# High and low halves in one stationary operand, and 512-column products in the second layer: a two-block network on one core

## The chip, the cores and the metric

The kernel runs on one core of a Trainium2 chip. The metric is the device time of one execution in microseconds; the time before is the median of three runs. The profile is one further execution, recorded instruction by instruction. Its engines are TensorE (PE, with its weight loads as PEld), VectorE (DVE), ScalarE (ACT), GpSimd (POOL) and SyncE (SP), which issues the loads.

## What is computed

Two blocks follow each other on 512 tokens of width 1024. The first has 16 extra meta tokens in front (528 rows) and two layers; the second has chunked attention over 8 heads, a gated recurrence, cross attention to a memory, and 32 routed experts. What the change touches, cut from the reference:

```python
for l in range(DEPTH):                       # first block, DEPTH = 2
    u = rms_norm(h, norm_w[l]) @ w_in[l]
    f_in, f_gate, p_in, p_gate, c_q, c_kv, k_r, a_gate = split(u)
    y_f, y_p = fourier_mix(f_in), pool_mix(p_in)
    y_a = mla_mix(c_q, c_kv, k_r, ...)       # k_r, 64 wide, is the rope key shared by 4 heads
    mix = concat(y_f*silu(f_gate), y_p*silu(p_gate), y_a*silu(a_gate))
    h = h + mix @ w_out[l]
...
probs = softmax(q @ k.T / 8 + bias)          # second block: 8 heads of 64 columns
out = probs @ v
```

## The kernel before

Every fp32 product is made of three TensorE products. An operand is split into a high part (rounded to the PE's input type) and a low part (what the rounding left), and `mm3` (L182) adds high x high, high x low and low x high in PSUM. Weights are split in `weights` (L162): ACT writes the high part at L176, POOL the low part at L177. Activations are split by `split` and `scaled_split` (ACT at L196 or L203, DVE at L197 or L204).

In the first block activations lie with features on partitions and tokens in the free dimension. `proj_g` computes one output tile of 128 features for all tokens in two halves. With all 528 tokens a half is 264 columns. In the second layer (`l == 1`) the results of the meta tokens are not used, so the queries, the gates and the output projection run over 512 tokens, in two halves of 256. With `small` the halves have one-bank tiles `p`, otherwise a two-bank tile `pp`; the generator hands control back every four steps of k, so that such projections can serve as fillers in the attention loop.

The input projection of a layer runs its column blocks in the order of `todo`: three query blocks, two key/value blocks, two pooling blocks (DVE then slides windows over them in `window`, L409 to L419), the rope keys (`None`), and two Fourier blocks `f`. For the rope keys `weights` loads the 64 columns twice, so that 128 output rows hold two equal copies, 48 products in all; one DVE instruction (L356) scales them out of PSUM, `rope` makes the swapped copy with four ACT copies (L311) and three DVE operations (L312 to L314), and `split` ends it (L196, L197). After that DVE scales the two Fourier blocks (L356), whose transposes (L554) are the next thing on PE.

In the second block the values are computed for all heads into four PSUM tiles and split into `vv`, one pair of high and low tiles for each 128 tokens. `outputs(h)` (L1002 on) multiplies a 128-column pair of heads with the transposed probabilities by `mm3`, for four blocks of keys with 512, 384, 256 and 128 columns, and copies the 64 rows of its own head out of PSUM with one ACT copy (L1013). Between the scores of one item and the transposes of the one before, the loop calls `fill`, which puts other projections on PE.

A scheduler orders the instructions of each engine when the program is built; an engine then executes its own in that order, and one that waits holds all behind it on its engine.

## Time and profile before

| what | before |
|---|---|
| median of 3 runs | 1425.4 us (1424.39 to 1425.71) |
| profiled execution, its own time | 1425.72 us |
| its span | 1423.9 us |
| PE busy | 1353.4 us, 95% of the span |
| DVE, ACT, POOL busy | 48%, 39%, 31% |

In time the first block takes the span up to about 522 us (the second layer starts at about 275 us), the second block's attention and cross attention up to about 890 us, and router and experts the rest. A row of the timeline gives the start in us from the beginning of the span, the duration in us, the engine, the source line, the operation, what is written and read, how many merged instructions, and in brackets how long the engine stood idle before it and who ended the wait. PE durations contain the passage through the array, so that successive products overlap: what a product takes in a row of them is read from the distance of starts, not from its duration.

### The profile page before, as it was taken

To read this page: it belongs to the slowest core of one execution; us is meant where nothing else is said; L and a number is where in the kernel's file an instruction comes from. 1 tells how busy PE (TensorE), PEld (TensorE's weight loads), DVE (VectorE), ACT (ScalarE), POOL (GpSimd) and SP (SyncE) were. 2 spreads that over 40 slices of the span, in tenths; PEclk is the share of its full clock that TensorE was granted. 3 is DMA by queue.
4 is the path that set the end of the run, shared out by engine and by line. 5 is a ranking of instruction groups with operands and counts; after the bars stand their busy time and mean duration, and the time that the engine had idled before them with its cause. 6 is when DMAs were issued, how large, how long until landed. Compare 5 with 4: busy or idle time off the path is not lost.

```text
span 1423.9 us, 21255 instructions
## 1 busy us (share of the span) xinstructions
PE 1353.4 (95%) x8236; PEld 1018.1 (71%) x8236; DVE 683.4 (48%) x1305; ACT 555.1 (39%) x1048; POOL 440.1 (31%) x363
## 2 busy tenths in 40 slices
PE   6999999999999999989999999979999999999996
PEld 5998999999899997767876788863454354354343
DVE  5656775455677636777766244252213123132224
ACT  5355554334555562667755344421111110111113
POOL 3432223743222488464477432512000000000002
PEclk9999999999999999999999999989999999999998
DMA  6321112332211242313345122959999999999994
GB/s 202 96 75 40 49 52 84 97 97 66 56 42 58 69 125 81 90 52 120 103 127 175 38 63 91 347 200 382 423 403 423 422 422 423 422 420 422 422 418 154
DMA packets 159288, 279.32 MB, mean 196 GB/s; under 512 B 15568, under 2 KB 127440, under 8 KB 135120
## 3 DMA queue, kind: packets, MB, share of 16 engines
q1 hardware_dynamic: 159184, 277.92, 53.0%
q8 instruction: 66, 1.08, 0.3%
q14 instruction: 38, 0.31, 0.1%
HBM read 275.79 MB, written 2.10 MB: 195 GB/s over the span
## 4 chain that ended last, share of the span: by engine, by line
PE 59%; DVE 7%; DMA 3%; ACT 2%; issue 1%; POOL 1%; DVEq 0%; SPq 0%; POOLq 0%; ACTq 0%
PE pga L1530 7%; PE pgb L1530 7%; PE pm L184 5%; PE pm L185 5%; PE pm L183 5%; PE pgs L1621 4%; PE pgz L1580 3%; PE pgy L1580 3%; PE pgs L1352 3%; PE p L183 2%; PE p L184 2%; PE p L185 2%; DMA ring<-in_expert_gate_w_dram 1%; DMA ring<-in_expert_up_w_dram 1%; DVE slab L197 1%
## 5 line engine op out<-in xcount | busy, mean ns | idle before, releaser
L177 POOL TENSOR_TENSOR wl<-wraw,wh 128x512 fp32r<-128x512 f32 (+1 forms) x248 | 328.1, 1332 | 457.1 <-ACT wh L176 425.2
L176 ACT ACTIVATE wh<-wraw 128x512 fp32r<-128x512 f32 (+1 forms) x248 | 150.6, 616 | 212.6 <-PE pm L184 49.8
L183 PE MATMUL pp<-slab,wh 128*128 128x264 f32 (+1 forms) x536 | 154.8, 290 | 7.6 <-ACT wh L176 6.8
L184 PE MATMUL pp<-slab,wh 128*128 128x264 f32 (+1 forms) x536 | 155.7, 291 | 2.9 <-DVE slab L204 2.7
L185 PE MATMUL pp<-slab,wl 128*128 128x264 f32 (+1 forms) x536 | 154.8, 289 | 1.0 <-POOL wl L177 1.0
L1788 POOL TENSOR_TENSOR ring<-xtok,sel 128x512 f32<-128x512 f32 x4 | 5.0, 1282 | 406.2 <-DVE xtok L1623 406.2
L185 PE MATMUL pm<-slab,wl 128*128 128x512 f32 (+1 forms) x320 | 121.5, 381 | 5.6 <-POOL wl L177 5.5
L184 PE MATMUL pm<-slab,wh 128*128 128x512 f32 (+1 forms) x320 | 120.9, 378 | 2.2 <-DVE slab L197 2.2
L183 PE MATMUL pm<-slab,wh 128*128 128x512 f32 (+1 forms) x320 | 121.1, 380 | 0.0
L183 PE MATMUL p<-slab,wh 128*128 128x264 f32 (+1 forms) x400 | 115.7, 289 | 3.3 <-DVE rs L247 1.6
L1530 PE MATMUL pga<-ring,xT 128*64 128x512 f32 x504 | 116.1, 596 | 0.0
L1530 PE MATMUL pgb<-ring,xT 128*64 128x512 f32 x512 | 113.7, 592 | 0.3 <-DMA ring<-in_expert_up_w_dram 0.3
L185 PE MATMUL p<-slab,wl 128*128 128x264 f32 (+1 forms) x400 | 113.1, 283 | 0.0
L184 PE MATMUL p<-slab,wh 128*128 128x264 f32 (+1 forms) x400 | 112.8, 282 | 0.0
L183 PEld LDWEIGHTS pp<-slab,wh 128*128 128x128 f32 x536 | 103.6, 194 | 8.0 <-ACT wh L176 6.8
L184 PEld LDWEIGHTS pp<-slab,wh 128*128 128x128 f32 x536 | 103.4, 193 | 4.7 <-DVE slab L204 4.2
L185 PEld LDWEIGHTS pp<-slab,wl 128*128 128x128 f32 x536 | 103.8, 194 | 1.5 <-POOL wl L177 1.5
L1530 PEld LDWEIGHTS pgb<-ring,xT 128*64 128x64 f32 x512 | 37.0, 137 | 73.6 <-issue 71.4
L1590 DVE SCALAR_TENSOR_TENSOR yl<-pgy,wcol,yh 128x512 fp32r<-128x512 f32 x16 | 12.0, 751 | 158.2 <-ACT yh L1589 158.2
L1530 PEld LDWEIGHTS pga<-ring,xT 128*64 128x64 f32 x504 | 35.4, 137 | 66.1 <-issue 65.6
L183 PEld LDWEIGHTS p<-slab,wh 128*128 128x128 f32 x400 | 75.5, 189 | 5.1 <-issue 1.7
L184 PEld LDWEIGHTS p<-slab,wh 128*128 128x128 f32 x400 | 75.4, 189 | 0.0
(412 smaller groups left out, 3007.6 us busy)
## 6 DMA issues: line engine op xcount, KB each, us to landing
ring<-in_expert_gate_w_dram SPq DMA_DIRECT2D x63, 1024.0 KB, 17.7
ring<-in_expert_up_w_dram SPq DMA_DIRECT2D x62, 1024.0 KB, 16.2
ring<-in_expert_down_w_dram SPq DMA_DIRECT2D x56, 1024.0 KB, 17.0
wraw<-in_w_in_dram SPq DMA_DIRECT2D x108, 256.0 KB, 2.9
wraw<-in_w_out_dram SPq DMA_DIRECT2D x48, 256.0 KB, 2.9
wraw<-in_xk_w_dram SPq DMA_DIRECT2D x16, 256.0 KB, 2.9
wraw<-in_xv_w_dram SPq DMA_DIRECT2D x16, 256.0 KB, 2.6
wraw<-in_xq_w_dram SPq DMA_DIRECT2D x16, 256.0 KB, 2.9
```

The source lines that it names most:

```text
L176: ACT(h, raw, AF.Copy)
L177: G.tensor_tensor(lo, raw, h.bitcast(F32), op=OP.subtract)
L183: mm(ps, lh, rh, start=first, stop=False)
L184: mm(ps, lh, rl, start=False, stop=False)
L185: mm(ps, ll, rh, start=False, stop=last)
L197: V.tensor_tensor(lo, x, h.bitcast(F32), op=OP.subtract)
L1352: mm(p, h3[:, i, 128 * k:128 * k + 128], sl_[i], start=i == 0 and z == 0, stop=i == 3 and z == 1)
L1530: mm(p[64 * z:64 * z + 64], xt[:, k, CAP * (q + z):CAP * (q + z) + 64], W(src, 2 * pr + z, k), start=k == 0, stop=k == KT - 1)
L1580: mm(ps[c // 512][64 * z:64 * z + 64, c % 512:c % 512 + n], hT_[:, k, 64 * z:64 * z + 64], W("d", 2 * pr + z, k, c, n), start=k == 0, stop ...
L1590: V.scalar_tensor_tensor(yl, p, w[:rows, 0:1], yh.bitcast(F32), op0=OP.mult, op1=OP.subtract)
L1621: mm(p, t[:, 128 * i:128 * i + 128], y, start=q == 0, stop=q == len(ys) - 1)
L1788: G.tensor_tensor(y[i][:, :512], xtok[:, i, :512], fnw[:, :512], op=OP.mult)
```

## The change

Three edits. First, `proj_g` computes a tile of 512 columns in one pass where the operand has 512 columns (`whole`), hands control back every two steps of k instead of four, and evacuates once. Second, the rope keys: `w_rope` loads the 64 columns once and writes high and low part side by side into one 128-column operand; each is multiplied with the high and the low activations, 32 products instead of 48, and the two halves of the result are added with three ACT copies and two DVE operations. Third, the values of the second block: high and low part of a head stand side by side in 128 columns, so `outputs` needs two products where it had three; the two halves of its result are added by an ACT copy and a DVE addition instead of the one ACT copy. `vv` is split by 16 instructions on 256 columns instead of 8 on 512.

```diff
             K = len(X)
-            n = (X[0][0].shape[1] - q0) // 2
+            n = X[0][0].shape[1] - q0
+            whole = n == 512
+            n, kk = (n, 2) if whole else (n // 2, 4)
...
-                    if k % 4 == 3 and k < K - 1:
+                    if k % kk == kk - 1 and k < K - 1:
                         yield
 
-            if small:
+            if whole:
+                p = p1t() if small else ppt()[:, 0]
+                yield from run(p, 0)
+                evac(p, lambda t: t)
+                yield
+            elif small:
...
+        def w_rope(l):
+
+            raw = wraw.tile([128, 512], F32, name="wraw").rearrange("p (k n) -> p k n", k=KT)
+            nc.sync.dma_start(raw, a["w_in"][l][:, 1664:1728].rearrange("(k p) n -> p k n", p=128))
+            ws = []
+            for q, nm in enumerate(("wh", "wl")):
+                t = wp.tile([128, 512], F32R, name=nm).rearrange("p (k z n) -> p k z n", k=4, z=2)
+                x = raw[:, 4 * q:4 * q + 4]
+                ACT(t[:, :, 0], x, AF.Copy)
+                G.tensor_tensor(t[:, :, 1], x, t[:, :, 0].bitcast(F32), op=OP.subtract)
+                ws += [t[:, k].rearrange("p z n -> p (z n)") for k in range(4)]
+            return ws
...
-            krh, krl = split(rope(inproj(None)))
+            kr = slab()
+            w = ahead(None)
+            p = ppt()
+            for hf in range(2):
+                for k, x in enumerate(X):
+                    for z in range(2):
+                        mm(p[:, hf, :HL], w[k], x[z][:, hf * HL:hf * HL + HL], start=k == 0 and z == 0,
+                           stop=k == KT - 1 and z == 1)
+            ACT(halves(kr)[64:], p[64:, :, :HL], AF.Copy)
+            ACT(kr[:64], kr[64:], AF.Copy)
+            V.tensor_tensor(halves(kr)[:64], p[:64, :, :HL], halves(kr)[:64], op=OP.add)
+            V.tensor_tensor(kr[:64], kr[:64], R1()[:64], op=OP.mult)
+            ACT(kr[64:], kr[:64], AF.Copy)
+            krh, krl = split(rope(kr))
...
-        vv = [scaled_split(pv[j], r12[:, j:j + 1], n=S) for j in range(4)]
+
+        vv = []
+        for j in range(4):
+            vv.append([slab(F32R, S) for _ in range(2)])
+            for q, t in enumerate(vv[j]):
+                tv = t.rearrange("p (e z c) -> p e z c", e=4, z=2)
+                scaled_split(pv[j][:, 256 * q:256 * q + 256].rearrange("p (e c) -> p e c", e=4), r12[:, j:j + 1],
+                             tv[:, :, 0], tv[:, :, 1])
...
-            c = slice(128 * pr, 128 * pr + 128)
             for j in range(4):
                 s = slice(384 * j + 128 * j, 384 * j + 512)
-                mm3(p[:, 128 * j:], vv[j][0][:, c], vv[j][1][:, c], th[:, s], tl[:, s], j == 0, j == 3)
+                v = vv[j][h // 4][:, 128 * (h % 4):128 * (h % 4) + 128]
+                mm(p[:, 128 * j:], v, th[:, s], start=j == 0, stop=False)
+                mm(p[:, 128 * j:], v, tl[:, s], start=False, stop=j == 3)
...
-            ACT(yat[pr][r], p[r], AF.Copy)
+            t = slab(n=S)
+            ACT(t[:64], p[64:], AF.Copy)
+            V.tensor_tensor(yat[pr][r], p[:64], t[:64], op=OP.add)
```

The order of DVE's instructions at the rope keys of the second layer, before; `slab` with `pp` is a scaling out of PSUM, and the last line but one is the two Fourier blocks:

```order
L418 TENSOR_TENSOR slab<-slab,tab_83 64x2x8
L419 TENSOR_TENSOR slab<-slab 64x2x8
L356 TENSOR_TENSOR slab<-pp,slab 128x528
L312 TENSOR_TENSOR slab<-slab,tab_83 128x528
L313 TENSOR_TENSOR slab<-slab,tab_83 128x528
L314 TENSOR_TENSOR slab<-slab 128x528
L197 TENSOR_TENSOR slab<-slab 128x528
L356 TENSOR_TENSOR slab<-pp,slab 128x528 x2
L197 TENSOR_TENSOR big<-pt,big 106x5x128
```

The same place in the changed kernel, where L319 to L321 are the lines of `rope` and L375 is what L356 was:

```order
L437 TENSOR_TENSOR slab<-slab,tab_83 64x2x8
L459 TENSOR_TENSOR slab<-pp,slab 64x528
L438 TENSOR_TENSOR slab<-slab 64x2x8
L460 TENSOR_TENSOR slab<-slab 64x528
L319 TENSOR_TENSOR slab<-slab,tab_83 128x528
L320 TENSOR_TENSOR slab<-slab,tab_83 128x528
L321 TENSOR_TENSOR slab<-slab 128x528
L197 TENSOR_TENSOR slab<-slab 128x528
L375 TENSOR_TENSOR slab<-pp,slab 128x528 x2
L197 TENSOR_TENSOR big<-pt,big 106x5x128 x2
```

The one scaling has become an addition (L459) and a scaling (L460) of 64 rows; both still stand behind the windows and ahead of the Fourier blocks.

DVE at the end of the first head of the second block, before; L197 is the last split of the head's transposed probabilities, L983 reads the next head's scores:

```order
L986 TENSOR_SCALAR slab<-slab,st_7488 128x128
L197 TENSOR_TENSOR ptl<-px,pth 128x4x128
L983 ISA slab,st_7525<-ps,slab 128x256
L983 ISA st_7525 128x1
L877 TENSOR_TENSOR slab<-pm,slab 128x512
```

The same place in the changed kernel (L1022 is what L983 was, L916 what L877 was):

```order
L1025 TENSOR_SCALAR slab<-slab,st_6902 128x128
L197 TENSOR_TENSOR ptl<-px,pth 128x4x128
L1055 TENSOR_TENSOR slab<-po,slab 64x512
L1022 ISA slab,st_6937<-ps,slab 128x256
L1022 ISA st_6937 128x1
L916 TENSOR_TENSOR slab<-pm,slab 128x512
```

The addition of `outputs` (L1055), which waits for PE's products and an ACT copy, stands ahead of the read of the next head's scores.

## Rows read from the trace of the kernel before

**Rows 1.** Page, part 1: busy us (share of the span) and instructions by engine.
```profile
PE 1353.4 (95%) x8236; PEld 1018.1 (71%) x8236; DVE 683.4 (48%) x1305; ACT 555.1 (39%) x1048; POOL 440.1 (31%) x363
```
**Rows 2.** Busy by stretch: PE, PEld, DVE, ACT, POOL, PEclk, DMA share, GB/s.
```profile
640.00:720.00 80.00, 75.64 (x469) 65.49 (x470) 58.43 (x172) 59.38 (x146) 36.22 (x34) 0.96 0.37 113
1000.00:1100.00 100.00, 100.00 (x491) 47.41 (x491) 25.91 (x50) 12.38 (x20) 0.00 (x0) 1.00 1.00 416
```
**Rows 3.** Groups by shape: products of 256 columns (xcount, busy us, mean ns).
```profile
L183 PE MATMUL p<-slab,wh 128*128 128x256 f32 x184 | 52.7, 287 | 1.6 <-DVE rs L247 1.6
L183 PE MATMUL pp<-slab,wh 128*128 128x256 f32 x156 | 44.1, 284 | 0.8 <-ACT slab L196 0.8
```
**Rows 4.** Timeline, DVE: evacuations that follow PE, 256, 512 and 264 columns.
```profile
492.62 0.69 DVE L641 TENSOR_TENSOR hT<-pp,hT 128x512 f32<-128x512 f32 x1 [0.93 <-PE pp L185]
...
515.29 0.69 DVE L641 TENSOR_TENSOR hT<-pp,hT 128x512 f32<-128x512 f32 x1 [3.01 <-PE pp L185]
...
780.25 0.69 DVE L1085 TENSOR_TENSOR hT<-hT,pm 128x512 f32<-128x512 f32 x1 [1.23 <-PE pm L185]
...
802.47 0.69 DVE L1085 TENSOR_TENSOR hT<-hT,pm 128x512 f32<-128x512 f32 x1 [3.32 <-PE pm L185]
...
250.99 0.71 DVE L641 TENSOR_TENSOR hT<-pp,hT 128x528 f32<-128x528 f32 x1 [2.57 <-PE pp L185]
...
268.50 0.71 DVE L641 TENSOR_TENSOR hT<-pp,hT 128x528 f32<-128x528 f32 x1 [2.46 <-PE pp L185]
```
**Rows 5.** Timeline, DVE, ACT, POOL and PE at the rope keys, second layer.
```profile
321.36 0.70 DVE L416 SCALAR_TENSOR_TENSOR slab<-slab 64x528 f32<-64x528 f32 x1
...
323.90 1.75 DVE L416 SCALAR_TENSOR_TENSOR slab<-slab 64x528 f32<-64x528 f32 x1
...
326.29 0.71 DVE L356 TENSOR_TENSOR slab<-pp,slab 128x528 f32<-128x528 f32 x1
329.66 0.71 DVE L312 TENSOR_TENSOR slab<-slab,tab 128x528 f32<-128x528 f32 x1 [2.67 <-ACT slab L311]
...
334.10 1.39 DVE L356 TENSOR_TENSOR slab<-pp,slab 128x528 f32<-128x528 f32 x2
...
327.03 2.60 ACT L311 ACTIVATE slab<-slab 32x528 f32<-32x528 f32 x4 [3.34 <-DVE slab L356]
...
322.30 2.78 POOL L177 TENSOR_TENSOR wl<-wraw,wh 128x512 fp32r<-128x512 f32 x2 [3.07 <-ACT wh L176]
...
334.86 0.76 PE L554 MATMUL pt<-tab,slab 128*106 128x128 f32 x5
```
**Rows 6.** Timeline, DVE and PE: the same place in the first layer.
```profile
80.84 1.42 DVE L356 TENSOR_TENSOR slab<-pp,slab 128x528 f32<-128x528 f32 x2
...
81.59 0.76 PE L554 MATMUL pt<-tab,slab 128*106 128x128 f32 x5
```
**Rows 7.** Timeline, PE: two long waits; then the stretches that follow them (as rows 2).
```profile
562.57 0.50 PE L185 MATMUL pm<-slab,wl 128*128 128x512 f32 x1 [2.29 <-POOL wl L177]
...
739.43 0.50 PE L183 MATMUL pm<-wh,slab 128*128 128x512 f32 x1 [2.18 <-DVE slab L204]
...
564.00:567.00 3.00, 3.00 (x9) 2.32 (x8) 2.93 (x3) 0.63 (x1) 3.00 (x3) 0.50 0.66 177
740.00:745.00 5.00, 5.00 (x23) 4.11 (x22) 0.48 (x1) 2.53 (x4) 4.83 (x5) 1.00 0.52 159
```
**Rows 8.** Timeline, PE and ACT: output of the second block's first head.
```profile
652.16 0.40 PE L184 MATMUL po<-ptl,slab 128*128 128x512 f32 x1
...
653.68 0.27 PE L185 MATMUL po<-pth,slab 128*128 128x128 f32 x1
...
653.99 0.59 ACT L1013 ACTIVATE slab<-po 64x512 f32<-64x512 f32 x1 [0.95 <-PE po L185]
654.49 0.50 ACT L984 ACTIVATE slab<-slab,st 128x256 f32<-128x256 f32 x1
```
**Rows 9.** Chain of waits: sixteen 512-column expert products with 64-column weights (start, us).
```profile
1017.60 3.43 PE pga L1530 x16
```

More of the change, by code (lines that the diff above doesn't have):

```diff
@@ L342, in ahead @@
                     if c not in ready:
-                        ready[c] = w_cols(l, c) if c is not None else weights(
-                            KT, [(0, w_in[:, 1664:1728]), (64, w_in[:, 1664:1728])])
+                        ready[c] = w_cols(l, c) if c is not None else w_rope(l)
                 return ready[c0]
```

## The prediction

> **What bounds the kernel now.** I read the page's busy times first: PE is busy for 95% of the span, twice as much as any other engine [rows 1]. The stretches then show that this holds for the experts, where PE has no gap and the loads run at full share, as for the second block's attention, where PE, DVE and ACT are all above 70% [rows 2]. So a product taken off PE shortens the run only where PE isn't waiting at that point for another engine, and for each of the three edits the question is what PE meets next. The busy times can't price a product, since a product's duration contains its passage through the array; for prices I took distances of starts in rows where PE never waits. Last I read who ends PE's waits at the places that the order moves.
>
> The experts are not touched, and their loads are issued by the program's own progress. What is won or lost before about 890 us moves them as a whole, one for one.
>
> **Edit 1, 512 columns in the second layer.** Products of 256 columns on weights: three lines with 184 in one-bank tiles and 156 in two-bank tiles each [rows 3], 3 x 340 = 1020; they become 510 of 512 columns. In the layer's output projection one tile of 48 such products follows the other every (515.29 - 492.62) / 4 = 5.67 us, 118.1 ns each; the second block's output projection, 24 products of 512 columns on weights of the same size, every (802.47 - 780.25) / 4 = 5.56 us, 231.5 ns each [rows 4]. So a pair costs 236.2 ns and its successor 231.5: 4.7 ns won, 510 x 4.7 = **-2.4 us**. Halving the number of products saves nearly nothing, because PE's time goes by columns. [...] The rows say 4.7 ns, and the sum goes by them.
>
> Fewer evacuations: a gate is evacuated once, not twice. That is DVE and ACT time in a layer where both have slack; I put it at nothing. The control points stay even: six products of 512 columns stand where twelve of 256 stood, so each filler step is as long as it was. The scheduler moves scores and transposes of the attention loop around; I can't price that from one trace and give it +-2 us.
>
> **Edit 2, rope keys.** On PE 16 products of 264 columns go in each layer. Their price is (268.50 - 250.99) / 3 / 48 = 121.6 ns [rows 4], so 1.9 us a layer, 3.9 us in all. But PE meets the Fourier transposes next, and these were just in time: in the second layer DVE starts the first Fourier evacuation at 334.10, half of a merged 1.39, and PE's transposes start at 334.86; in the first layer 80.84 and 81.59 [rows 5, 6]. DVE, not PE, is last there already. It comes from the windows without a pause into the key's evacuation at 326.29, then waits 2.67 for four ACT copies, does the rope and only then the Fourier blocks [rows 5]. The order of the changed kernel keeps this and lengthens it. The two ACT copies out of PSUM are free (the Fourier products take 96 x 0.1216 = 11.7 us up to the transposes at 334.86, so the key's products end at about 323.2, now 321.3, and DVE is through with the windows at 326.3). Then instead of one evacuation of 0.71 stand an addition (0.71, as L356), a scaling (0.70, as L416 on 64 rows) and, before the four swapped copies can start, one more ACT copy (2.60 / 4 = 0.65 [rows 5]): +1.4 us on the chain that releases the transposes. Against that: while POOL splits weights, DVE's operations stretch (L416 takes 0.70, but 1.75 beside L177 [rows 5]). The key's POOL work is halved and its operand takes one buffer less, so some of the next splits start before the windows. I take 0.9 of the 1.4 as given back. The transposes then start 0.5 us later than before, though PE is there 1.9 us earlier: no gain, **+0.5 us** in each layer, **+1.0**. The bounds: +1.4 a layer if nothing is given back, and the whole -1.9 if DVE is through early.
>
> That leaves PE idle for about 1.9 + 0.5 = 2.4 us at a place where it had no wait. [...]
>
> **Edit 3, values of the second block.** For each head 4 of 12 products go, one of each width, 1280 columns. Ten distances from 652.16 to 653.68 cover 3200 columns [rows 8], 0.475 ns a column, so 0.61 us a head and 4.9 us for eight. In their place comes a DVE addition of about 0.7 us (0.71 for L356). It stands in DVE's queue and waits for PE's last product and the ACT copy (0.59 [rows 8]). In four of eight heads (the first, third, fifth and seventh) it stands ahead of the read of the next head's scores, and exp, division and transposes of that item wait behind it. Before, that exp started at 654.49, behind the copy at 653.99 on ACT [rows 8]; now it is copy (653.99 - 0.61 + 0.59 = 653.97), addition (654.7), read of the scores (0.42, an estimate between the copy's 0.59 and half of it), 655.1: 0.6 later. PE has other projections between, and the new order puts a few more products ahead of those transposes. So between -0.6 and +0.6 for these four, and I take -0.3 each. For three heads the addition stands behind the reads: -0.6 each. In the last head the output is on the chain to the next projection, and addition and saved products cancel: 0. Sum -1.2 - 1.8 = **-3.0 us**, bounds -4.9 and +0.6.
>
> Splitting `vv` by 16 shorter instructions costs ACT and DVE about 0.5 us, on the way to the wait that ends at 562.57 [rows 7]; a memset that DVE waits for moves forward in POOL's queue. I let these cancel, +-0.5.
>
> **The sum.** -2.4 + 1.0 + 1.6 - 3.0 = -2.8 us. The profiled execution took 1425.72 us, 0.3 above the median of the runs. 1425.4 - 2.8 = 1422.6, rounded down to **1422.5 us**: just at 0.2%, about what a measurement of this kernel can tell from no change. The case's own range is the two unknown signs of the order (2 us), the clock (1.6) and the DVE additions (1 to 2): 1419.5 to 1425.5.
>
> **The rivals.**
> *The cover holds.* If the windows end some 2 us earlier than I think, all products removed count: -2.4 - 3.9 - 4.9 = -11.2, 1414.2 us; half of it gives 1418. For it: PE's share. Against it: transposes and evacuation 0.05 us apart in both layers. Chance 0.15.
> *DVE becomes the bound, slower.* Both layers stall by the whole chain (+2.8) and drop the clock twice (+3.3), and the additions hold the softmax in the four heads (+0.6) and bring one more clock drop (+1.6): -2.4 + 2.8 + 3.3 + 0.6 + 1.6 = +5.9, 1431.3 us. [...] For it: DVE at 58 of 80 us in that attention [rows 2]. Against it: the fillers that the order puts in between. Chance 0.15.
> *Columns cheaper in long products.* With weights of 64 columns 512 columns take 3.43 / 16 = 214 ns [rows 9]. If the layer's products ran so, edit 1 would give 510 x 22 = 11.2 us, 8.8 more than summed: 1413.7. Against it: the weights are 128 wide, and rows of that kind exist. Chance 0.03. [...]
> *The first edit does nothing*: 512 columns as dear as two halves, 1425.0. Chance 0.05.
>
> **How the numbers follow.** The forecast case has 0.62, half of it on either side of 0.2%. Faster by over 0.2%: 0.30 + 0.15 + 0.03 = 0.48. Within: 0.32 + 0.05 = 0.37. Slower: 0.15. The range leaves out the whole-cover end and the far half of the slower case: 1416.5 to 1428.5.
>
> **What would show it.** In the changed profile: output tiles of the second layer every 5.56 us (edit 1); PE waiting 2 to 3 us for a DVE evacuation ahead of both pairs of Fourier transposes, and a clock below 1.00 behind one of them (edit 2); DVE waiting for the ACT copy at the additions, and PE's waits for DVE in the heads no longer than before by more than 0.6 us each (edit 3). No wait at the transposes would make me wrong on the fast side; longer waits of PE in the attention of either block, which the new order could bring anywhere, on the slow side.

## The result, and the profile after

The changed kernel took 1442.05 us (median of 4 runs, 1436.02 to 1444.34), the kernel before 1424.89 beside it (4 runs, 1423.63 to 1425.71): ratio 1.0112, 95% interval 1.0084 to 1.0140, so some 16 us slower. The forecast was 1422.5, at most 1428.5. On a second chip (run e13 below) the ratio was 1.0091 (1.0076 to 1.0106), 13 us. Below, "+5.4 us" and the like are a run's ratio times 1426, about what the kernel before took beside it.

First the page of the changed kernel, busy us by engine, which answers to [rows 1]:

```profile
PE 1356.1 (94%) x7662; PEld 992.7 (69%) x7662; DVE 681.7 (47%) x1297; ACT 558.0 (39%) x1046; POOL 441.8 (31%) x363
```

PE issues 574 products fewer than in [rows 1] and is busy 2.7 us longer. Of these, 510 were only merged into longer ones, but 64 (edits 2 and 3, 8.8 us by the prediction's prices) went without a replacement. So the products that are left took longer, as products of this kernel do at a lower clock: before, those of 512 columns start every 0.43 us from 564.30 to 566.86 us, at a granted clock of 0.50, and every 0.23 us from 741.85 to 743.91, at 1.00. The waits of PE and the clock behind them come next. Waits of PE in the changed kernel (line, what was waited for: us in all, times, longest):

```profile
PE pm L185 <- POOL wl L177: 7.7, 3, 3.4
...
PE ps L1017 <- DVE st L1022: 7.0, 7, 2.7
...
PE pt L586 <- DVE slab L375: 5.5, 2, 2.8
PE pm L184 <- DVE slab L197: 4.2, 5, 2.4
```

The same view of the kernel before:

```profile
PE pm L185 <- POOL wl L177: 5.5, 2, 3.2
PE pm L184 <- DVE slab L197: 3.5, 7, 0.7
...
PE ps L978 <- DVE st L983: 3.1, 2, 2.7
```

L586 are the Fourier transposes (L554 before), which had no wait before; L1017 are the second block's scores (L978 before), waiting for the read of an earlier score tile on DVE. The clock in the changed kernel in five stretches of the trace (start:end, length, PE busy, granted clock, DMA share, GB/s):

```profile
82.00:85.00 3.00, 2.86 (x13) 0.53 0.66 173
338.00:341.00 3.00, 3.00 (x9) 0.53 0.63 165
684.00:688.00 4.00, 3.21 (x17) 0.79 0.55 159
700.00:704.00 4.00, 3.52 (x13) 0.50 0.01 2
780.00:784.00 4.00, 3.55 (x8) 0.50 0.62 183
```

The kernel before has a granted clock of 1.00 in the first four of these stretches, and in the place of its program that answers to the last. In windows of 1 us over both spans the clock reads 1.00 or 0.50 everywhere but where it changes; below, a stretch at 0.50 is one of half clock. Adding up (1 - clock) over the whole span gives an estimate of the time lost in these stretches: 22 us before and 38 us after, of which 10 and 26 lie ahead of 900 us. Not all of it counts, since PE doesn't set the end everywhere, but the difference of 16 us is nearly as large as the 18.4 us between the two spans.

Where the time goes is read from the starts of PE's products, whose durations overlap (0.39 us each, at starts 0.23 us apart, in the row of 512-column products from 741.85 us before). The table gives lengths in us: the first layer (up to the transposes of the next norm's statistics), the second layer (up to the second block's first product), values and recurrence (up to the first scores of the chunked attention), from these to the attention's first output product, that attention (first to last output product), last output to norm (to the transposes of its statistics), and the output projection (from there to the cross-attention's first scores). Each row is one profiled execution, and some of these lie well off the median of their kernel's runs: e14's took 1428.0 us (median 1436.2), e9's 1429.2 (1433.8), e6's 1421.3 (1424.1) and e18's 1428.3 (1426.5). The experiments follow below.

| kernel | layer 1 | layer 2 | values, recurrence | scores to output | attention | output to norm | projection |
|---|---|---|---|---|---|---|---|
| before | 282.4 | 238.4 | 110.9 | 19.4 | 102.8 | 6.0 | 54.3 |
| changed | 284.5 | 237.9 | 113.2 | 19.6 | 110.2 | 7.5 | 58.8 |
| changed, second chip (e13) | 285.4 | 237.9 | 113.6 | 17.5 | 108.9 | 7.5 | 58.7 |
| changed, PE kept busy (e14) | 280.0 | 236.2 | 113.1 | 17.8 | 105.4 | 7.5 | 56.3 |
| edit 2, PE kept busy (e5) | 283.8 | 240.5 | 112.2 | 17.5 | 102.9 | 6.0 | 54.3 |
| edit 3 alone (e4) | 282.6 | 238.3 | 112.2 | 17.4 | 105.9 | 7.5 | 56.2 |
| edit 3 alone again (e16) | 282.4 | 240.0 | 112.2 | 17.4 | 105.9 | 7.5 | 56.2 |
| edit 3, no addition (e6) | 281.5 | 239.7 | 112.2 | 17.4 | 99.5 | 6.0 | 54.3 |
| edit 3, unrelated addition (e18) | 282.6 | 238.4 | 112.1 | 17.6 | 103.2 | 6.0 | 55.7 |
| edit 3, late addition (e9) | 280.7 | 238.4 | 112.0 | 17.6 | 105.6 | 7.5 | 56.4 |

The last three columns are from rows such as these, PE's timeline in the changed kernel (start, us, line, tile, what ended the idle time before):

```profile
655.16 0.50 PE L1048 MATMUL po<-pth,slab 128*128 128x512 f32 x1
...
765.39 0.27 PE L1049 MATMUL po<-ptl,slab 128*128 128x128 f32 x1
...
772.92 0.65 PE L759 MATMUL px<-tab,rstd 128*128 128x128 f32 x4 [0.77 <-POOL rstd L753]
...
831.68 0.37 PE L183 MATMUL ps<-slab 128*128 128x256 f32 x1
```

The first layer's length varies between executions of the same code: from 280.7 to 282.6 us in the rows with the old rope keys, and 283.8 and 280.0 in e5 and e14, which both have edit 2 and PE kept busy. The time that half clock takes there varies too: 3.4 us in the kernel before and in e18, 1.7 in e16, none in e14. In the second block the kernel before and e5 have the same order of instructions, and take 110.9 and 112.2 us in values and recurrence, and 19.4 and 17.5 behind them; behind them half clock lost 3.4 us in the kernel before (638 to 646 us) and none in e16 and e18, with 17.4 and 17.6. The attention of the old code repeats within 0.2 us (102.7 to 102.9 in the kernel before, e2, e3 and e5) where no such stretch falls into it.

### The profile page after: what moved, and what is told of

It reads as the page before. It is cut to its first block, busy times and chain, and to the rows that moved or that the text cites. A ratio compares the mean times of both kernels' runs of the same rounds, so it can differ in the third digit from the quotient of the medians.

```text
span 1442.3 us, 20086 instructions
## 1 busy us (share of the span) xinstructions
PE 1356.1 (94%) x7662; PEld 992.7 (69%) x7662; DVE 681.7 (47%) x1297; ACT 558.0 (39%) x1046; POOL 441.8 (31%) x363
## 5 line engine op out<-in xcount | busy, mean ns | idle before, releaser
L177 POOL TENSOR_TENSOR wl<-wraw,wh 128x512 fp32r<-128x512 f32 (+1 forms) x244 | 327.0, 1348 | 456.6 <-ACT wh L176 433.5
L176 ACT ACTIVATE wh<-wraw 128x512 fp32r<-128x512 f32 (+1 forms) x244 | 148.2, 616 | 224.3 <-PE pm L184 51.5
L183 PE MATMUL pp<-slab,wh 128*128 128x264 f32 (+1 forms) x426 | 132.5, 312 | 7.1 <-ACT wh L176 7.1
L184 PE MATMUL pp<-slab,wh 128*128 128x264 f32 (+1 forms) x426 | 133.0, 313 | 2.8 <-DVE slab L204 2.8
L185 PE MATMUL pp<-slab,wl 128*128 128x264 f32 (+1 forms) x426 | 132.6, 312 | 0.9 <-POOL wl L177 0.9
L184 PE MATMUL pm<-slab,wh 128*128 128x512 f32 (+1 forms) x320 | 123.5, 387 | 3.4 <-DVE slab L197 2.9
L183 PE MATMUL pm<-slab,wh 128*128 128x512 f32 (+1 forms) x320 | 122.7, 387 | 1.1 <-ACT slab L196 1.1
L183 PE MATMUL p<-slab,wh 128*128 128x264 f32 (+1 forms) x308 | 101.3, 329 | 3.2 <-DVE slab L197 1.9
L185 PE MATMUL p<-slab,wl 128*128 128x264 f32 (+1 forms) x308 | 98.7, 320 | 0.0
L184 PE MATMUL p<-slab,wh 128*128 128x264 f32 (+1 forms) x308 | 98.5, 320 | 0.0
L183 PEld LDWEIGHTS pp<-slab,wh 128*128 128x128 f32 x426 | 82.7, 195 | 10.5 <-ACT wh L176 7.3
L184 PEld LDWEIGHTS pp<-slab,wh 128*128 128x128 f32 x426 | 82.7, 194 | 7.6 <-DVE slab L204 4.0
L185 PEld LDWEIGHTS pp<-slab,wl 128*128 128x128 f32 x426 | 82.8, 195 | 4.9 <-POOL wl L177 1.6
L185 PEld LDWEIGHTS pm<-slab,wl 128*128 128x128 f32 x320 | 62.8, 196 | 20.7 <-POOL wl L177 9.9
L184 PEld LDWEIGHTS pm<-slab,wh 128*128 128x128 f32 x320 | 62.6, 196 | 15.9 <-DVE slab L197 4.8
```

The source lines that it names most:

```text
L176: ACT(h, raw, AF.Copy)
L177: G.tensor_tensor(lo, raw, h.bitcast(F32), op=OP.subtract)
L183: mm(ps, lh, rh, start=first, stop=False)
L184: mm(ps, lh, rl, start=False, stop=False)
L185: mm(ps, ll, rh, start=False, stop=last)
```

## The experiments

**Each edit alone.** In the texts of this group theory A holds that the loss lies at certain places and so belongs to certain edits, and rival B that the edits act on the second block through each other or through any shift ahead of it.

e1, edit 1 alone:
```diff
+            n, kk = (n, 2) if whole else (n // 2, 4)
...
+            if whole:
+                p = p1t() if small else ppt()[:, 0]
+                yield from run(p, 0)
```


> The kernel before with edit 1 alone (products of 512 columns in the second layer). Theory A (the loss of the changed kernel can be taken apart by place, and edit 1 is innocent): at the end of the second layer the changed kernel stands 1.4 us behind, the first layer's rope keys having cost 2.1 us by the first Fourier product (96.02 before, 98.14 after); two layers of that make 4.2, so edit 1 gives 1.4 - 4.2 = -2.8 us, 1422 us. Rival B (the waits in the second block come from the moved meeting of loads and splits, which any edit ahead of them brings): slower than before, up to 1436 us, with half-clock stretches in the attention of the second block. The forecast's own term was -2.4.

Measured: ratio 0.9984 (0.9973 to 0.9995), -2.3 us. Theory A holds. Edit 1 is the only one of the three edits that gains, and the only complete version run here that is faster than the kernel before by more than its interval.

e2, edit 2 alone:
```diff
-            krh, krl = split(rope(inproj(None)))
...
+            w = ahead(None)
...
+            ACT(kr[:64], kr[64:], AF.Copy)
+            V.tensor_tensor(halves(kr)[:64], p[:64, :, :HL], halves(kr)[:64], op=OP.add)
```


> The kernel before with edit 2 alone (rope keys). Theory A: PE waits 2.7 us for the Fourier evacuation in each layer, as in the changed kernel (2.77 and 2.69), with a granted clock of 0.5 for about 3 us behind each; +2.1 us a layer, +4.2 in all, 1429 us, and the attention of the second block as before. Rival B: 1425 +- 1 at the second block's start and further losses of several us in its attention. A third case: the waits come but the clock stays at 1.00, then +0.5 a layer, 1426 us.

Measured: 1.0038 (1.0027 to 1.0049), +5.4 us, with two waits at the transposes, 5.5 us together, and the attention of the second block as before. Theory A holds.

e4, edit 3 alone:
```diff
+                mm(p[:, 128 * j:], v, th[:, s], start=j == 0, stop=False)
+                mm(p[:, 128 * j:], v, tl[:, s], start=False, stop=j == 3)
...
+            ACT(t[:64], p[64:], AF.Copy)
+            V.tensor_tensor(yat[pr][r], p[:64], t[:64], op=OP.add)
```


> The kernel before with edit 3 alone (second block's values side by side, 8 products and an addition for each head). Theory A: it carries nearly all of the loss, 18.4 - 1.4 = 17 us in the profiled execution, by PE's waits for the scores' read on DVE (7.0 us in seven waits there, 3.1 in two before) and for the last head's output, with half clock behind them: 1436 to 1442 us. Rival B: without the shift that edits 1 and 2 bring, less than +6 us: below 1431 us. The forecast's own term was -3.0.

Measured: 1.0041 (1.0028 to 1.0054), +5.8 us; on the second chip (e16) 1.0049 (1.0036 to 1.0061), +7.0. Theory A falls: it is a clear loss, but not the 17 us. Rival B's bound, +6, is just met on the first chip and missed on the second. The waits for the scores' read are there (6.8 us in six).

**Edit 2: the chain or the clock.** e3 puts the rope keys behind the Fourier blocks:
```diff
-            todo = [1024, 1152, 1280, 1408, 1536, 512, 640, None, 0, 128,
+            todo = [1024, 1152, 1280, 1408, 1536, 512, 640, 0, 128, None,
+            f = [inproj(128 * m) for m in range(2)]
             kr = slab()
...
-            f = [inproj(128 * m) for m in range(2)]
```


> Edit 2 alone, with the two Fourier blocks projected and evacuated ahead of the rope keys, so that the key's 32 products stand between the Fourier products and the transposes and its additions come behind the Fourier evacuations on DVE. Theory A (DVE's queue ahead of the transposes is what costs, not the products or copies as such): no wait over 0.3 us at the transposes, clock 1.00 behind them, 3.9 us of PE's products saved, 1421 us. Rival: the rope chain is late for the first scores instead, and the wait only moves: 1425 to 1429 us.

Measured: 1.0043 (1.0030 to 1.0056), +6.1 us, no better. PE starts the transposes without a wait, as theory A wanted, but ACT's queue then holds the rope's four swapped copies (L311), the second Fourier evacuation (L196) and only then the next weights' split (L176), and PE waits for that. PE and ACT at this place in e3:

```profile
87.81 0.40 PE L183 MATMUL pp<-slab,wh 128*128 128x264 f32 x1 [1.28 <-ACT wh L176]
...
83.87 2.61 ACT L311 ACTIVATE slab<-slab 32x528 f32<-32x528 f32 x4
86.50 0.70 ACT L196 ACTIVATE big<-pt 106x640 fp32r<-106x640 f32 x1
87.23 1.05 ACT L176 ACTIVATE wh<-wraw 128x384 fp32r<-128x384 f32 x2
```

A wait of 1.28 us and one of 0.33 behind it took the place of the 2.77, and the clock fell at 88 to 94 us all the same, 1.7 us lost; the first layer ended 1.5 us later than in the kernel before. In the second layer the same wait is 1.45 us long, and the clock stays at 1.00 behind it (the second line is a stretch, columns as above):

```profile
342.72 0.39 PE L183 MATMUL pp<-slab,wh 128*128 128x256 f32 x1 [1.45 <-ACT wh L176]
...
342.00:346.00 4.00, 2.93 (x22) 1.00 0.18 51
```

So the rival holds: the wait moved, and the longer chain fits neither place without one.

e5 leaves edit 2 as it is and fills the wait:
```diff
                 p = ptt()
+                for r in range(16 if m == 0 else 0):
+                    mm(p[:, :HL], Q[0][0][:, :128], X[r % KT][0][:, :HL], start=True, stop=True)
```


> Edit 2 alone, with 16 products of 264 columns that nobody reads put on PE right ahead of the first pair of Fourier transposes in each layer (work added; the order of everything else is that of edit 2 alone). In edit 2 alone PE stands idle there for 2.77 and 2.69 us, and the granted clock is 0.50 for about 3.4 us behind, 1.7 us lost each. Theory A (the clock falls because PE stands idle, and the fall costs by itself): the 1.95 us of products fit into the idle time, the transposes start at the same time, no fall at 82 and 338 us, 3.4 us faster than edit 2 alone, 1428.5 us. Rival (the fall has another cause, such as the load of the chip at that moment): as edit 2 alone or up to 1 us slower, 1432 to 1433 us.

Measured: 1.0008 (0.9998 to 1.0017), +1.1 us where edit 2 alone had +5.4. Nothing else in the order of any engine differs. Edit 2 alone, the idle stretch and the one behind it, first layer (columns as above):

```profile
79.00:82.00 3.00, 0.95 (x8) 1.00 0.25 57
83.00:86.00 3.00, 3.00 (x17) 0.51 0.65 177
```

and with the unread products:

```profile
79.00:82.00 3.00, 3.00 (x25) 1.00 0.24 54
83.00:86.00 3.00, 3.00 (x27) 1.00 0.66 173
...
339.00:342.00 3.00, 3.00 (x28) 1.00 0.67 172
```

The transposes start at the same time (82.72 and 82.84), and PE does 27 products instead of 17 in the 3 us behind them. The clock fell to 0.51 behind the idle stretch and stayed at 1.00 where PE was kept busy. So the two falls follow from PE's idle time here, and they cost about 4 us of edit 2's 5.4 (on two chips, each within about 1.5). Theory A holds.

**Edit 3: products, addition, or its place.** e6 leaves out copy and addition of the low part:
```diff
-            t = slab(n=S)
-            ACT(t[:64], p[64:], AF.Copy)
-            V.tensor_tensor(yat[pr][r], p[:64], t[:64], op=OP.add)
+            ACT(yat[pr][r], p[:64], AF.Copy)
```


> Edit 3 alone, with the addition and the copy of the upper half left out: one copy of 64 rows by ACT, as in the kernel before, so the part from the low values is missing from the result. Theory A (the 8 products and the new layout are a gain, and what costs is the addition, with the order that it brings about): 4.9 us of products saved, less what PE waits anyway in that attention, 1421 to 1424 us, with the waits for the scores' read back at 3.1 us. Rival (PE's shorter stretches between the reads make it wait for DVE just as long): 1426 us or more, with PE's waits for the scores at 6 us, as with the additions.

Measured: 0.9986 (0.9978 to 0.9995), -2.0 us. Theory A holds. The attention takes 99.5 us, 3.3 less than before: the products saved are worth most of the 4.9 us forecast. All of the loss is in the addition and what comes with it, 7.8 us from here to e4. What comes with it includes a new order: without the addition the scheduler places the attention's instructions on PE, DVE and ACT differently from e4 in 30 or more places each, and no run keeps the order and leaves out the addition alone.

What the addition does directly is seen in the changed kernel at the output of its third head; PE, ACT and DVE (L1048 and L1049 output products, L1054 copy, L1055 addition, L1022 the scores' read):

```profile
682.69 0.27 PE L1049 MATMUL po<-ptl,slab 128*128 128x128 f32 x1
...
684.70 0.50 PE L1017 MATMUL ps<-slab 128*128 128x512 f32 x1 [1.57 <-DVE st L1022]
...
683.00 0.59 ACT L1054 ACTIVATE slab<-po 64x512 f32<-64x512 f32 x1 [1.00 <-PE po L1049]
...
683.62 0.68 DVE L1055 TENSOR_TENSOR slab<-po,slab 64x512 f32<-64x512 f32 x1 [1.82 <-ACT slab L1054]
684.23 0.41 DVE L1022 CUSTOM_DVE_ANT_0 slab<-ps,slab 128x256 f32<-128x256 f32 x1
```

DVE stands still for 1.82 us until products and copy are through, adds for 0.68, and only then reads the 256-column scores; PE, whose next scores need that tile, waits 1.57. In edit 3 alone the same rows stand at 678 to 680 us with the same 1.82 and 1.57.

e9 moves the addition behind that read:
```diff
-            V.tensor_tensor(yat[pr][r], p[:64], t[:64], op=OP.add)
+            late.append(lambda: V.tensor_tensor(yat[pr][r], p[:64], t[:64], op=OP.add))
...
                 e = scores(h, i)
+                if i == 2 and late:
+                    late.pop()()
```


> Edit 3 alone, with each head's addition issued behind the next head's third scores, so that on DVE it stands behind the reads of the 256- and 384-column scores in all heads but one (there behind the first of the two); in edit 3 alone it stood ahead of both in four heads and between them in three. Theory A (what edit 3 costs is this place: DVE waits 1.8 to 3.6 us for copy and products ahead of the addition, the reads of the next scores wait behind it, and PE for their two buffers): PE's waits for the scores' read fall from 6.8 us to about the 2.7 of the single wait at 638 us, no half clock at 694 to 702, last head's chain +1.3 us as before: 1426 - 4.9 + 1.3 + 1 = 1423.5 us. Rival (the addition's and copy's own time is the cost, wherever they stand): 1429 to 1432 us.

Measured: 1.0048 (1.0032 to 1.0065), +6.8 us: no gain, theory A falls. DVE no longer stands still ahead of the additions. Its waits for the copy in the attention of edit 3 alone, then with the late addition:

```profile
DVE slab L1023 <- ACT slab L1022: 13.0, 7, 3.6
```

```profile
DVE slab L1024 <- ACT slab L1023: 1.2, 1, 1.2
```

Yet the attention is as long, 105.6 us. PE's waits go to other places. Edit 3 alone, from 645 to 757 us:

```profile
PE ps L985 <- DVE st L990: 4.1, 5, 1.6
...
PE px L1001 <- DVE slab L993: 2.1, 4, 0.9
```

with the late addition, same stretch:

```profile
PE px L1001 <- DVE slab L993: 5.3, 8, 1.0
PE ps L985 <- DVE st L990: 2.6, 6, 0.9
```

L1001 are the transposes of the weights of attention, which wait for their division on DVE (L993). What is taken from the reads is put on the divisions, and more: PE's waits in the attention add up to 7.6 us without additions (e6), 9.7 in edit 3 alone and 12.1 here. Edit 3 alone also loses 3.4 us to the lower clock there (at 694 to 701 us), e6 and e9 nothing. These 3.4 us are not simply a cost on top: the changed kernel with PE kept busy (e14, below) has the order of edit 3 in the attention and no such stretch, and takes 105.4 us with 11.9 us of waits.

e18 asks whether it is DVE's time as such. To e6 it adds an addition for each head that waits for nothing:
```diff
             ACT(yat[pr][r], p[:64], AF.Copy)
+            t = slab(n=S)
+            V.tensor_tensor(t[:64], vv[0][0][:64].bitcast(F32), vv[1][0][:64].bitcast(F32), op=OP.add)
```


> Edit 3 without copy and addition of the low part, as before (that part is missing from the result), but with an addition of the same size on DVE for each head, of two operands that have long been ready, so that it waits for nothing. The stretch from the first to the last output product took 99.4 us without additions and 105.9 with those of edit 3. Theory A (DVE's own time sets the pace there, 8 x 0.7 us come on top wherever they stand): 104 to 105.5 us, 1429 us. Rival (what costs is that the addition waits for copy and products, with the reads behind it): 99.5 to 101 us, 1424 to 1425 us.

Measured: 1.0003 (0.9994 to 1.0012), +0.4 us, 2.4 more than without additions and 5.4 to 6.6 less than with those of edit 3. The attention takes 103.2, of which 1.7 are a stretch of half clock at 738 to 742 us that e6 doesn't have. It lies between the two texts, by its time nearer to the rival (1424 to 1425), by the attention nearer to theory A (104 to 105.5). In four heads these additions stand ahead of the next head's reads, as in edit 3; they never wait, but beside POOL's operations some take 0.9 to 1.8 us instead of 0.7. So DVE's time and the new order alone cost 2.0 to 3.7 us in the attention (without and with the stretch of half clock), against 6.4 in edit 3; the rest goes with the wait for products and copy, or with the order of edit 3. Taking away DVE's standing still alone, in e9, did not take away that rest.

The rest of that cost is behind the attention. The last head's output goes through copy and addition to the norm, 7.5 us instead of 6.0, in every kernel with the addition and in none without. And the projection takes 1.9 us longer. Part of it is that the norm now meets POOL: in e6 the three scalings of the rows (L1089) and POOL's split (L177) stand one behind the other,

```profile
757.80 2.08 DVE L1089 SCALAR_TENSOR_TENSOR slab<-slab,cols 128x512 f32<-128x512 f32 x3
...
756.30 1.28 POOL L177 TENSOR_TENSOR wl<-wraw,wh 128x512 fp32r<-128x512 f32 x1
```

in edit 3 alone they stand side by side, and the same three operations take half as long again:

```profile
765.37 3.11 DVE L1091 SCALAR_TENSOR_TENSOR slab<-slab,cols 128x512 f32<-128x512 f32 x3
...
766.32 1.61 POOL L177 TENSOR_TENSOR wl<-wraw,wh 128x512 fp32r<-128x512 f32 x1 [2.42 <-ACT wh L176]
```

The kernel before has 2.08 here too. That is 1.0 us of the 1.9. Edit 3 alone also loses 1.7 us to the lower clock at 769 us, which e6 and the kernel before don't have; e18 has that stretch and the short 2.08, and its projection is 1.4 us longer than e6's. How the 1.9 us divide between the two is not shown.

**Do the edits add up?** Alone they give -2.3 + 5.4 + 5.8 = 8.9 us, the changed kernel gave 16. e7 has edits 1 and 3, e8 edits 2 and 3, e15 edits 1 and 2, each by the hunks of the diff named.

> Edits 1 and 3 without the rope keys. Medians so far: edit 1 alone -2.2, edit 2 alone +6.2, edit 3 alone +5.2 us, together 9.2, while all three give +17. Theory B (additive but for what all three bring together): 1426 + 3.0 = 1429 us. Theory C (the missing 8 us are in edits 1 and 3 together: with edit 1 the second block is entered with weights later in their buffers): 1435 us or more, with more than three half-clock stretches between 560 and 790 us.

> Edits 2 and 3 without the long products. Theory B (additive): 1426 + 11.4 = 1437.4 us. Theory C (the missing 8 us are in edits 1 and 3): the same 1437 us. Theory D (they are in edits 2 and 3): 1443 us or more. The half-clock stretches between 560 and 790 us: three in edit 3 alone, six in the changed kernel.

> Edits 1 and 2 without the values. Additive: -2.2 + 6.2 = +4.0 us over the kernel before. If the part that the single edits don't explain is in this pair: +8 us or more.

Measured: e7 1.0044 (1.0031 to 1.0057), +6.3 us against a sum of 3.5; e8 1.0111 (1.0094 to 1.0128), +15.8 against 11.2 (both between their texts); e15 1.0025 (1.0016 to 1.0033), +3.6 against 3.1, additive. e15 was run with the changed kernel itself and edit 3 alone on one chip:

> The changed kernel itself, on the same chip as the three that follow. Theory A (the three edits interact: falls of the clock in the second block that none of them brings alone): +16 to 17 us over the kernel before, as on the first chip, though the single edits add up to 9.2. Rival B (the edits add up, and the first chip's four runs lay high): +9 us, 1435 us.

> Edit 3 alone again, on the same chip: +5.2 us over the kernel before if the chips agree; with +4.0 for edits 1 and 2 together the sum for the changed kernel is +9.2. More than +7 would say that the chips differ by as much as the part in question.

Measured: the changed kernel +13.0 us (10.8 to 15.1), e15 and e16 together 3.6 + 7.0 = 10.6 (each within about 1.5). The missing part shrinks from 7 to 2.4 us, which these intervals don't tell from nothing. So much of the first gap may have been the chip and the few runs; a remainder of some 2 to 5 us, if there is one, comes with edits 2 and 3 together (e8). The profiled executions put such a surplus into the attention, which takes 110.9 us in e8, 110.2 and 108.9 in the changed kernel, but 105.9 in edit 3 alone, in the same order of instructions; the stretches of half clock below go with it.

**Both costs taken out of the changed kernel.** e11, and again as e14 on the chip of e13, is the changed kernel with the unread products of e5; e12 has the late addition of e9 as well.

> The changed kernel with nothing changed but 16 products of 264 columns that nobody reads ahead of the first pair of Fourier transposes in each layer. Theory A (the clock's fall there costs by itself, as in edit 2 alone, where it took 4.9 us): 1442 - 3.4 to 5 = 1437 to 1438.5 us. Rival (the falls of the clock in the second block depend on when it is entered, and 3 us of shift changes them by more than that): anything from 1431 to 1442 us, with other places of half clock between 560 and 790 us than in the changed kernel.

> The changed kernel with the unread products ahead of the Fourier transposes again, now beside the changed kernel on one chip. Theory A: 8 to 9 us faster than the changed kernel (1433 against 1442 on two chips), more than the 5 us that the same products gave in edit 2 alone. Rival B: 5 us faster.

> The changed kernel with both: the unread products ahead of the Fourier transposes and the late addition. Theory A (these two places hold the loss; edit 2 then costs its 0.5 us a layer, edits 1 and 3 gain 2.2 and 2.5): 1426 + 1 - 2.2 - 2.5 = 1422.3 us, some 20 us faster than the changed kernel. Rival (a third cause, such as the weights' arrival in the second block, holds the part of the 17 us that the single edits don't add up to, about 6): 1428 us or more.

Measured: e11 1.0048 (1.0029 to 1.0066), +6.8 us; e14 1.0071 (1.0058 to 1.0084), +10.1, where the changed kernel on the same chip had +13.0 (by the medians 1436.2 and 1440.2); e12 1.0053 (1.0037 to 1.0068), +7.6. So the unread products are worth 3 to 4 us beside it, as the two falls are, and the late addition nothing. e11 lies in its rival's range, e14 is nearer to rival B, and theory A of e12's text falls by 13 us; what the third cause of its rival would be is not shown. The executions with a profile show one thing more. Two stretches of the attention with PE kept busy (e14), where the changed kernel above has a clock of 0.79 and 0.50:

```profile
684.00:688.00 4.00, 3.66 (x28) 1.00 0.00 0
700.00:704.00 4.00, 2.96 (x26) 1.00 0.51 151
```

From this attention on the order of instructions is the same in e4, e7, e8, e11, e14 and the changed kernel. It takes 105.4 us without a stretch of half clock (e11 and e14), 105.9 and 107.0 with 3.4 us lost to them (e4, e7), 108.9 with 5.1 (the changed kernel in e13), and 110.2 and 110.9 with 6.8 (the changed kernel above, e8). Whether the clock falls behind a given wait is thus not fixed by the order, and what such stretches cost is not fixed by their length alone: with 3.4 us lost the attention is 0.5 to 1.6 us longer, with 6.8 lost 4.8 to 5.5.

**Trying to gain.** e10, edits 1 and 3 with the late addition:

> Edits 1 and 3 with the late addition, without the rope keys: meant to beat both kernels. Theory A: -2.2 for edit 1 and -2.5 for edit 3 with the late addition, 1421 to 1422 us. Rival: as edits 1 and 3 (1431.5 us) or with half of that loss, 1428 us.

Measured: 1.0025 (1.0012 to 1.0038), +3.6 us, the rival. e17, edit 1 with unread products in three waits that the kernel before has as well:
```diff
+                if (c, k) == (2, 4):
+                    unread(ps_, "ps", 8)
+                if (c, k) == (11, 3):
+                    unread(ps_, "ps", 12)
...
+            if (h, i) == (0, 2):
+                unread(px_, "px", 9)
```


> Edit 1 alone, with products that nobody reads put into three waits of PE that the kernel before has too: 8 of 512 columns (1.85 us) into the wait for the low weights at 559 us (2.29), 12 (2.8 us) into that at 623 us (3.2), 9 (2.1 us) into the wait for the scores' read at 635 us (2.7). Theory A (idle time of PE brings the falls of the clock, each fall costs 1.7 us or more where PE sets the end): no half clock behind these three waits, 1.7 to 5 us faster than edit 1 alone, -4 to -7 us against the kernel before, 1419 to 1422 us: faster than both. Rival (PE waits for POOL's splits there anyway, so the faster products only wait longer at the next one): as edit 1 alone, -2 us.

Measured: 0.9996 (0.9987 to 1.0005), -0.6 us, 1.7 less gain than edit 1 alone: the rival. The falls behind the first two waits are gone, but others stand in their place, 3.4 us long at 572 and 6.8 at 637 us. After the first PE meets POOL's statistics (L728) earlier and waits for them longer. Edit 1 alone, then e17:

```profile
573.57 0.43 PE L734 MATMUL px<-tab,rstd 128*128 128x128 f32 x2 [1.15 <-POOL rstd L728]
```

```profile
572.36 0.69 PE L734 MATMUL px<-tab,rstd 128*128 128x128 f32 x2 [2.73 <-POOL rstd L728]
```

The third set came to stand behind the wait that it was meant to fill (at 641.8 us, the wait ends at 638.4) and was 3.1 us of work on top. Here preventing two falls gave nothing: the time won went into the next wait for another engine, and the clock fell behind that.

## Why the prediction was wrong

**Edit 1: right.** -2.4 forecast, -2.3 (-0.7 to -3.8) measured in e1. Output tiles of the second layer in the changed kernel, as in [rows 4]:

```profile
494.70 0.69 DVE L673 TENSOR_TENSOR hT<-pp,hT 128x512 f32<-128x512 f32 x1
...
517.02 0.69 DVE L673 TENSOR_TENSOR hT<-pp,hT 128x512 f32<-128x512 f32 x1 [3.00 <-PE pp L185]
```

(517.02 - 494.70) / 4 = 5.58 us a tile, 5.56 forecast. The rivals of cheap long columns and of no effect are out.

**Edit 2: the place and the wait right, the clock one fall short.** PE meets the transposes while DVE is at the longer rope chain, first layer of the changed kernel (L459 addition, L460 scaling, L318 swapped copies, L375 Fourier evacuations), to be held against [rows 6]:

```profile
79.08 0.29 PE L185 MATMUL pp<-slab,wl 128*128 128x264 f32 x1
82.14 1.31 PE L586 MATMUL pt<-tab,slab 128*106 128x128 f32 x5 [2.77 <-DVE slab L375]
...
71.69 0.70 DVE L459 TENSOR_TENSOR slab<-pp,slab 64x528 f32<-64x528 f32 x1
...
72.62 0.70 DVE L460 TENSOR_TENSOR slab<-slab 64x528 f32<-64x528 f32 x1
76.73 0.71 DVE L319 TENSOR_TENSOR slab<-slab,tab 128x528 f32<-128x528 f32 x1 [3.41 <-ACT slab L318]
...
81.39 1.31 DVE L375 TENSOR_TENSOR slab<-pp,slab 128x528 f32<-128x528 f32 x2
```

The transposes start 82.14 - 81.59 = 0.55 us later than before, 0.5 forecast, and e5 leaves +1.1 us for the two layers, +1.0 forecast. The idle time came to 2.77 and 2.69 us, 2.4 forecast. The clock term failed by a fall: the sum's +1.6 us was my estimate for one fall in one of the two layers, and no run shows it. The clock of the changed kernel fell in both layers, to 0.53 over the 3 us from 82 and from 338 us, and to 0.50 at 84 and at 340 us on the second chip, and in e5 keeping PE busy gave back 5.4 - 1.1 = 4.3 us for the two.

**Edit 3: the step that failed.** -3.0 forecast, bounds -4.9 and +0.6; +5.8 and +7.0 measured, outside both. By its terms:
- The saved products, -4.9: -3.3 in the attention (e6).
- The additions, "between -0.6 and +0.6" for four heads and pure gain for three: 105.9 - 99.5 = +6.4 us in the attention, their new order included. I had priced the read's delay at one head, [rows 8], where the copy sat just ahead of the exp, and had the fillers of PE hide it. What the step left out is that DVE, in its order, stands still until products and copy are through: 13.0 us ahead of seven additions, 1.82 of them at the third head, and 1.0 to 1.2 in each of the three heads that I had counted as gain. PE, with two tiles for scores, then waits 1.57 us. That the standing still is the whole price is not shown: e9 removes 11.8 of these 13.0 us, and the attention is as long.
- The last head, 0 because "addition and saved products cancel": +1.5. The saved products lie ahead of the copy only as far as PE sets the pace there; copy and addition are on the chain in full.
- The projection: no term. +1.9, in part from the norm's scalings beside POOL's splits.
- The values' split, 0 +-0.5: no net loss. The wait that [rows 7] shows at 2.29 us is 3.38 in edit 3 alone, and values and recurrence grew by 1.2 us, but the stretch behind them, up to the first output product, is 2.0 us shorter. There the kernel before lost 3.4 us to the lower clock, edit 3 alone nothing.

```profile
566.55 0.49 PE L185 MATMUL pm<-slab,wl 128*128 128x512 f32 x1 [3.38 <-POOL wl L177]
```

Together -3.3 + 6.4 + 1.5 + 1.9 - 0.8 = +5.7 us, near the +5.8 measured.

**The sum and the chances.** With the measured terms, -2.3 + 5.4 + 5.8 to 7.0, the sum is +9 to +10, and the changed kernel measured +13 and +16. The slower rival, 1431.3 at 0.15, had the right places, DVE's chains and the clock behind them, but gave the additions +0.6 and one fall. No run shows its terms for the clock, +3.3 and +1.6: the two falls at the transposes were worth the 4.3 us of e5, and in the attention half clock took 3.4 us in edit 3 alone, 5.1 and 6.8 in the changed kernel. The waits of DVE ahead of the additions, which it left out, were the sign that these were more than 0.7 us each. The sentence on what would make me wrong on the slow side, waits of PE in the attention of either block, is what came.

**Still open.** Why an addition behind the reads (e9) costs the attention as much as one ahead of them, though an unrelated one (e18) costs less; how much of the additions' price is the scheduler's new order and not the additions; what sets whether the clock falls behind a given wait; and whether the last 2 to 5 us are an interaction of edits 2 and 3.

## What to carry to other kernels

Do not price an operation that is added to an in-order queue by its own duration: also look, for each place where it stands, at how long the engine stands still until its inputs are there, and at what the new order does to the rest. Here 0.7 us of addition cost 1 us a head, on an engine that was busy for only 58 of 80 us [rows 2], and moving the addition to a place with ready inputs did not help. Look also at what PE meets behind the products that are taken from it: here DVE was last at the transposes, PE stood idle there for 2.77 and 2.69 us, the clock behind fell to 0.51 (e2), and a saving that I had put at 3.9 us became a loss of 5.4. Unread products in such a wait are a cheap test of that. They gave back 4.3 us in e5, and nothing in e17, where PE only waited longer at the next place, 2.73 us instead of 1.15.

## What was not expected of the hardware

- A single wait of 2.7 us (e2), and one of 1.28 with one of 0.33 behind it (e3), were followed by a stretch of half clock that lost another 1.7 us; other stretches lost 3.4 (699 to 707 us in the changed kernel) or 5.1 (778 to 789).
- The clock fell behind both waits at the transposes in e2 (0.51), e15 (0.50 at 84 and at 340 us) and both executions of the changed kernel (0.53, and 0.50 at 84 and at 340 us). A wait of 2.18 us [rows 7] was followed by a clock of 1.00 before; in the changed kernel the same wait, 2.10 us at 749 us, was followed by a fall (0.68 in the stretch below), and in e14 a wait of 2.09 at this place was not (1.00 from 744 to 756 us). In these three the length of the one wait doesn't decide it.

```profile
752.00:756.00 4.00, 4.00 (x14) 0.68 0.58 167
```
